# Queries, keys and one mixer's softmax weights: copied bit for bit into float32r row buffers and turned as float32r, with the norm tasks ahead of others

## The chip, the cores and the metric

The kernel runs on one core of one Trainium2 chip. The metric is the device time of one execution in microseconds; the time before is the median of three runs.

## The reference, cut to what matters

One layer of a decoder on a sequence of 512 tokens (S) with a model width of 1024 (D). A combined input projection yields queries, keys and values for two attention mixers of 4 heads with 128 channels each, and gates. Queries and keys pass a per-head RMS norm with a gain and a rotary embedding. The first mixer (DSA) lets each query attend to the 128 keys that a small indexer ranks highest; the second (MoBA) is causal over blocks of 256, which at this size is plain causal attention. Both outputs are projected, gated by sigmoids, added and projected again; a SwiGLU feed-forward layer with 2816 hidden channels follows. Everything is float32.

```python
q_a = apply_rope(rms_norm(q_a.reshape(B, S, DSA_HEADS, HEAD_DIM), g_q_dsa[l]), cos_h, sin_h)
k_a = apply_rope(rms_norm(k_a.reshape(B, S, DSA_HEADS, HEAD_DIM), g_k_dsa[l]), cos_h, sin_h)
o_a = dsa_attention(q_a, k_a, v_a, q_i, k_i, w_i)
q_b = apply_rope(rms_norm(q_b.reshape(B, S, MOBA_HEADS, HEAD_DIM), g_q_moba[l]), cos_h, sin_h)
k_b = apply_rope(rms_norm(k_b.reshape(B, S, MOBA_HEADS, HEAD_DIM), g_k_moba[l]), cos_h, sin_h)
o_b = moba_attention(q_b, k_b, v_b)
# inside both mixers, for every head and block of queries:
#   p = softmax(q @ k.T * scale + mask);  o = p @ v
```

## The kernel before, in words

Large products run on TensorE as float32r in three parts (high times high, high times low, low times high), because every operand is split into a rounded float32r tile and its remainder. The scores (`q @ k.T`) and `p @ v` run as plain float32.

**Queries and keys.** A projection leaves 128 tokens by 512 channels (4 heads) in a PSUM bank. `raw_done` (line 736) has ScalarE copy it into an SBUF tile `raw` of the tag `g` and spawns a task `post` (line 703). There are 16 such tasks: the names `kb`, `qb` (MoBA), `qa`, `ka` (DSA) times 4 blocks of tokens. `post` takes the squares' sums on ScalarE, the rotary embedding on VectorE, the power -1/2 on GpSimd and 4 scalings on ScalarE; then TensorE turns the 4 blocks of 128x128 of `raw` into a PSUM tile `pstr` with float32 transposes (identity `ident` as the moving operand, `raw` as the weights), and ScalarE copies the result into the tile `qk[name]` of the tag `K`.

**Heads.** `head(br, i, h)` (line 881) is one head of mixer `br` (1 is MoBA, 0 is DSA) for the block `i` of 128 queries; its keys reach to the end of that block, so its width is (i+1)*128. There are 16 per mixer. A score product goes to the PSUM tile `pss`; VectorE adds the mask; ScalarE takes the exponential into a tile `p` of the tag `s`; VectorE inverts the sum; ScalarE scales `p`; TensorE turns its i+1 blocks with float32 transposes into `pstr`; ScalarE copies that into `pT`; TensorE multiplies with the values into `pspv`; ScalarE and VectorE store the output in two parts.

**Float32r transposes that are there already.** `flip` (line 777), for the indexer's queries and keys: tiles that ScalarE and VectorE wrote as float32r are turned with `identr`, 4 blocks per call, 8 calls. `ident` is the same tile as `identr`, read as float32.

**The order.** Instructions on TensorE, ScalarE, VectorE and GpSimd run in the order in which the program emits them. A planner writes that order: `Clocks` (line 54) keeps an estimated time for each engine and for each tile. The main stream `drive` (line 586) emits the projections' products; after nearly every triple of products it calls `step` (line 503), which continues every waiting task whose needs are met at the planned time of TensorE. A need is a tile (ready time plus 0.25 us, `when`, line 489), a free buffer of a tag (`room`) or a named event. Tasks are tried in the order of their rank (lower first, 2 by default, in order of spawning within a rank). The main stream goes through MoBA's values, its queries, DSA's queries, keys and values, the gates (16 tiles of the tag `g`), then the two mixers' output projections. These need `attn1` and `attn0`, that is, all heads of a mixer.

**Buffers.** There are 16 tiles of `g`, 4 of `K`, 3 of `s`, 2 of `pT`, 2 banks of `pstr`, 1 each of `pss` and `pspv`.

**DMA.** Weights are loaded on SyncE's queue (`wload`, line 184 issues them), in the order of the tasks. GpSimd's queue issues copies later in the kernel. ScalarE's queue issues none.

Of the kernel before, what the change touches and what calls it, by code (L numbers as in the profile page):

```python
# [23 lines left out]
F32 = mybir.dt.float32  # L24
F32R = mybir.dt.float32r
# [4 lines left out]
P = 128  # L30
S = 512
# [3 lines left out]
HD = 128  # L35
NH = 4
# [81 lines left out]
def layer(ctx, tc, x, vecs, w_mod, w_in, gvecs, w_br_dsa, w_br_moba, w_out, w_gate_up, w_down, cosh, sinh, cosi, sini, out):  # L118
    nc = tc.nc
    ck = Clocks()  # L120
    te, se, ve, ge = (Noted(e, ck) for e in (nc.tensor, nc.scalar, nc.vector, nc.gpsimd))
# [15 lines left out]
    def taken(tag, tile):  # L137

        if free:
            times = free[tag]  # L140
            first = min(times)
            times.remove(first)
            tag_of[tile.tensor.name] = tag
            ck.last[tile.tensor.name] = (first, None)
        return tile

    def done(*tiles):
        for tile in tiles:
            name = tile.tensor.name
            free[tag_of.pop(name)].append(ck.last[name][0])  # L150

    def t(tag, shape, dt=F32):
        uid[0] += 1
        return taken(tag, reg.tile(shape, dt, name=f"{tag}_{uid[0]}", tag=tag, bufs=NB[tag]))

    def small(shape, dt=F32, bufs=4, tag=None):
        uid[0] += 1
        tag = tag or "m" + "_".join(str(v) for v in shape)
        return sm.tile(shape, dt, name=f"{tag}_{uid[0]}", tag=tag, bufs=bufs)
# [3 lines left out]
    def ps(tag, shape=(P, 512), dt=F32):  # L163
        uid[0] += 1
        return taken("ps" + tag, pp.tile(list(shape), dt, name=f"ps{tag}_{uid[0]}", tag="ps" + tag, bufs=NPB[tag]))
# [67 lines left out]
    identr = cp.tile([P, P], F32R, name="identr")  # L233
    ident = identr.bitcast(F32)
# [13 lines left out]
    def rstd_of(ms, width):  # L248

        r = small([P, width])  # L250
        ve.tensor_scalar(r, ms, EPS, None, op0=ALU.add)
        ge.tensor_tensor(out=r, in0=r, in1=mhalf[:, :width], op=ALU.pow)
        return r
# [232 lines left out]
    def room(tag, n=1):  # L486
        return lambda: sorted(free[tag])[n - 1] if len(free[tag]) >= n else None
# [9 lines left out]
    def spawn(gen, slack=2.0, rank=2, on=busy):  # L497
        tasks.append([gen, (), slack, on, rank])
        tasks.sort(key=lambda task: task[4])
# [46 lines left out]
    def need_room(tag):  # L546
        pump(lambda: free[tag])
# [126 lines left out]
    def gain_tables(g):  # L674
        cg = t("cg", [P, NT, HD])
        sg = t("cg", [P, NT, HD])
        hd = HD // 2
        gv = gains[:, g:g + 1, :]
        ve.tensor_tensor(out=cg, in0=cosd, in1=gv.to_broadcast([P, NT, HD]), op=ALU.mult)
        ve.tensor_tensor(out=sg[:, :, 0:hd], in0=sind[:, :, 0:hd],  # L680
                         in1=gv[:, :, hd:].to_broadcast([P, NT, hd]), op=ALU.mult)
        ve.tensor_tensor(out=sg[:, :, hd:], in0=sind[:, :, hd:],
                         in1=gv[:, :, 0:hd].to_broadcast([P, NT, hd]), op=ALU.mult)
        return cg, sg

    def rope(src, cos, sin, heads, d):

        u = t("gu", [P, heads, d])
        hd = d // 2
        ve.tensor_tensor(out=u[:, :, 0:hd], in0=src[:, :, hd:d], in1=sin[:, :, 0:hd], op=ALU.mult)  # L690
        ve.tensor_tensor(out=u[:, :, hd:d], in0=src[:, :, 0:hd], in1=sin[:, :, hd:d], op=ALU.mult)
        yield
        ve.tensor_tensor(out=src, in0=src, in1=cos, op=ALU.mult)
        ve.tensor_tensor(out=src, in0=src, in1=u, op=ALU.add)
        done(u)


    m1 = cp.tile([P, 256], F32, name="m1")
    sqj = m1[:, :HD]
    tabs = {}  # L700
    qk = {}

    def post(name, g, i, raw):
        if not i:
            yield room("cg", 2), room("K")
            tabs[name] = gain_tables(g)
            qk[name] = t("K", [P, NH, S])
            ready.add("tab" + name)
        yield "tab" + name, raw, room("gu")
        if name == "kb" and i >= 2:  # L710
            yield "idx", room("gu")
        cg, sg = tabs[name]
        ss = small([P, NH])
        for h in range(NH):
            se.activation(sqj, raw[:, h, :], AF.Square, scale=HD ** -0.5, accum_out=ss[:, h:h + 1])
        for _ in rope(raw, cg[:, i:i + 1, :].to_broadcast([P, NH, HD]), sg[:, i:i + 1, :].to_broadcast([P, NH, HD]),
                      NH, HD):
            yield ss, cg, sg
        r = rstd_of(ss, NH)
        yield raw, r  # L720
        for h in range(NH):
            se.activation(raw[:, h, :], raw[:, h, :], AF.Copy, scale=r[:, h:h + 1])
        yield raw, room("pstr")
        pt = ps("tr", (P, NH, P))
        for h in range(NH):
            te.transpose(pt[:, h, :], raw[:, h, :], ident)
        se.copy(qk[name][:, :, i * P:(i + 1) * P], pt)
        done(pt, raw)
        ready.add(f"{name}{i}")
        if all(f"{name}{j}" in ready for j in range(NT)):  # L730
            ready.add(name)
            done(*tabs[name])
            if name == "ka":
                done(cosd, sind, gains)

    def raw_done(name, g):
        def fin(i, acc):
            need_room("g")
            raw = t("g", [P, NH, HD])
            se.copy(raw, acc.rearrange("p (h d) -> p h d", h=NH))  # L740
            spawn(post(name, g, i, raw))
        return fin

    vals = {}
# [136 lines left out]
    def head(br, i, h):  # L881
        if br:
            yield "qb", "kb", "vb"
            q, k, v, mask = qk["qb"], qk["kb"], vals["vb"], cmask[:, (NT - 1 - i) * P:]
        else:
            yield ("index", "qa", "ka", "va", "started1") + ((f"bias{i}",) if i else ())
            q, k, v, mask = qk["qa"], qk["ka"], vals["va"], bias[i]
        w = (i + 1) * P
        sl = slice(i * P, (i + 1) * P)
        yield q, k, v, mask, room("pss"), room("s")  # L890
        s_ps = ps("s")
        te.matmul(s_ps[:, :w], q[:, h, sl], k[:, h, :w], start=True, stop=True)
        p = t("s", [P, S])
        st = small([P, 4], tag="att")
        nm, z, rz = (st[:, q:q + 1] for q in range(3))

        ve.tensor_tensor_reduce(out=p[:, :w], in0=s_ps[:, :w], in1=mask, op0=ALU.add, op1=ALU.min, scale=-SCALE,
                                scalar=-LOW, accum_out=nm)
        done(s_ps)
        yield st, p  # L900
        se.activation(p[:, :w], p[:, :w], AF.Exp, bias=nm, scale=-1.0, accum_out=z)
        yield p
        ve.reciprocal(rz, z)
        yield st
        se.activation(p[:, :w], p[:, :w], AF.Copy, scale=rz)
        yield p, room("pstr"), room("pT")
        pt = ps("tr")
        for j in range(i + 1):
            te.transpose(pt[:, j * P:(j + 1) * P], p[:, j * P:(j + 1) * P], ident)
        pT = t("pT", [P, S])  # L910
        se.copy(pT[:, :w], pt[:, :w])
        done(pt, p)
        if br not in outs:
            yield room("O", 2)
            outs[br] = [t("O", [P, NH, S], F32R) for _ in range(2)]
            ready.add(f"started{br}")
        yield pT, room("pspv")
        oh, ol = outs[br][0][:, h, sl], outs[br][1][:, h, sl]
        o_ps = ps("pv", (P, P))
        for j in range(i + 1):  # L920
            te.matmul(o_ps, v[:, j, h * HD:(h + 1) * HD], pT[:, j * P:(j + 1) * P], start=(j == 0), stop=(j == i))
        se.copy(oh, o_ps)
        done(pT)
        yield outs[br][0]
        ve.tensor_tensor(out=ol, in0=o_ps, in1=oh.bitcast(F32), op=ALU.subtract)
        done(o_ps)
        heads.remove((br, i, h))
        if not any(b == br for b, _, _ in heads):
            ready.add(f"attn{br}")
            done(vals["vb" if br else "va"], qk["qb" if br else "qa"], qk["kb" if br else "ka"])  # L930
            if not heads:
                done(cmask, bias[NT - 1])
# [97 lines left out]
    landed = [0.0]  # L1030
# [859 lines left out]
    with tc.manual_schedule(engines=engines):  # L1890
# [20 lines left out]
        for br, i, h in list(heads):  # L1911
            spawn(head(br, i, h), slack=2.5)
# [58 lines left out]
```

## Time and profile before

| what | value |
|---|---|
| time, median of three runs | 767.47 us (767.23 to 768.8) |
| the profiled execution | 767.38 us, of which the span from first to last instruction is 765.6 us |
| TensorE busy | 756.6 us (99%), 3884 products |
| VectorE busy | 603.6 us (79%) |
| ScalarE busy | 413.1 us (54%) |
| GpSimd busy | 62.1 us (8%) |
| granted TensorE clock | 1.000 |
| DMA | 137.10 MB, mean 179 GB/s |

The span is cut by engine: the share of an engine is the time in which at least one of its instructions is running. Products on TensorE overlap, so a group's mean duration is longer than the spacing of its instructions; the spacing of starts is what TensorE's time is made of. Nearly all instructions bear line 111, which is the helper that notes them for the planner, so groups are told apart by the tiles they write and read: `out<-in`, for a product first the moving operand, then the weights. A name without a number stands for all tiles of that tag.

### The profile page before, as it was taken

The page shows a single profiled execution, that of the slowest core. Times are in us where ns is not written, and L with a number is a line of the kernel's source. Part 1 is how long each engine was busy: PE and PEld are TensorE (multiplying, and loading weights), DVE is VectorE, ACT ScalarE, POOL GpSimd, SP SyncE. Part 2 cuts the span into 40 slices and gives each one's busy share as a digit, 9 for nine tenths or more (in the row PEclk, how much of TensorE's full clock was granted, in tenths as well). Part 3 has the DMA queues.
Part 4 walks back from the last instruction along what each step waited for, and adds up shares of the span by engine and source line. Part 5 has one row for each costly group of instructions (what it writes and reads, how often), then busy time and mean ns, then how long its engine had stood idle before and what let it go on. Part 6 is the DMA issues. An engine that isn't in the chain of part 4 may idle for free.

```text
span 765.6 us, 10985 instructions
## 1 busy us (share of the span) xinstructions
PE 756.6 (99%) x3884; PEld 639.2 (83%) x3884; DVE 603.6 (79%) x1183; ACT 413.1 (54%) x887; POOL 62.1 (8%) x91
## 2 busy tenths in 40 slices
PE   7999999999999999999999999999999999999998
PEld 6887888888788887888888988889999998888886
DVE  6974889989799796436967897878788856997896
ACT  6763686869877666643534443444444432554431
POOL 2000012011012000000000000000011020012100
PEclk9999999999999999999999999999999999999999
DMA  9976343542126455534450146744566679579882
GB/s 311 347 215 228 97 167 83 146 133 57 51 65 210 125 153 179 176 92 129 147 157 1 56 148 200 236 164 133 182 204 186 196 250 379 186 264 407 309 310 82
DMA packets 87921, 137.10 MB, mean 179 GB/s; under 512 B 9008, under 2 KB 49272, under 8 KB 87228
## 3 DMA queue, kind: packets, MB, share of 16 engines
q1 hardware_dynamic: 80076, 105.75, 44.0%
q0 software_dynamic: 7792, 30.67, 11.2%
q8 instruction: 30, 0.49, 0.3%
q14 instruction: 23, 0.19, 0.1%
HBM read 117.52 MB, written 18.88 MB: 178 GB/s over the span
## 4 chain that ended last, share of the span: by engine, by line
PE 95%; SPq 2%; DVE 1%; DMA 1%; issue 0%; ACT 0%; ACTq 0%
PE psacc L111 62%; PE pstr L111 11%; PE pspv L111 11%; PE pss L111 11%; SPq L184 1%; DMA K<-in_w_mod_dram 1%; DVE V L111 1%; DVE s L111 1%; SPq L213 0%; SPq L222 0%; ACT gu L111 0%; ACT H L111 0%; SPq L206 0%; ACT acol L111 0%; ACT mcol L111 0%
## 5 line engine op out<-in xcount | busy, mean ns | idle before, releaser
L111 DVE TENSOR_TENSOR wl<-st,wh 128x1024 fp32r<-128x1024 f32 (+1 forms) x98 | 113.6, 1160 | 42.9 <-ACT wh L111 33.6
L111 PE MATMUL psacc<-wh,H 128*128 128x512 f32 x384 | 126.4, 400 | 0.9 <-ACT H L111 0.9
L111 ACT CAST wh<-st 128x1024 fp32r<-128x1024 f32 (+1 forms) x98 | 97.6, 998 | 49.4 <-DMA st<-in_w_gate_up_dram 20.3
L111 PE MATMUL psacc<-H,wh 128*128 128x512 f32 x384 | 124.1, 404 | 0.0
L111 PEld LDWEIGHTS psacc<-wh,H 128*128 128x128 f32 x384 | 72.0, 188 | 16.4 <-ACT H L111 1.4
L111 PEld LDWEIGHTS psacc<-H,wh 128*128 128x128 f32 x384 | 70.0, 188 | 15.3 <-issue 2.7
L111 PE MATMUL psacc<-H,wl 128*128 128x512 f32 x192 | 75.1, 391 | 0.0
L111 PE MATMUL psacc<-H,O 128*128 128x256 f32 (+1 forms) x465 | 72.3, 296 | 0.0
L111 PE MATMUL psacc<-wl,H 128*128 128x512 f32 x192 | 71.0, 390 | 0.0
L111 PEld LDWEIGHTS psacc<-H,O 128*128 128x128 f32 x465 | 64.0, 191 | 2.7
L111 POOL TENSOR_TENSOR m<-m,mhalf 128x4 f32<-128x4 f32 (+1 forms) x24 | 28.6, 1193 | 390.8 <-DVE m L111 356.8
L111 PE MATMUL psacc<-K,O 128*128 128x256 f32 x288 | 43.4, 283 | 0.0
L111 PEld LDWEIGHTS psacc<-H,wl 128*128 128x128 f32 x192 | 36.0, 188 | 7.9
L111 PEld LDWEIGHTS psacc<-wl,H 128*128 128x128 f32 x192 | 36.1, 188 | 6.7
L111 PE MATMUL pss<-H,wh 128*128 128x512 f32 x128 | 39.5, 390 | 0.0
L111 PE MATMUL pspv<-H,wh 128*128 128x512 f32 x128 | 39.5, 390 | 0.0
L111 PE MATMUL psacc<-O,wh 128*128 128x512 f32 x128 | 39.4, 389 | 0.0
L111 PEld LDWEIGHTS psacc<-K,O 128*128 128x128 f32 x288 | 38.4, 191 | 0.0
L111 ACT ACTIVATE s<-s,att 128x256 f32<-128x256 f32 (+3 forms) x64 | 34.2, 562 | 4.6 <-DVE att L111 4.4
L111 ACT CAST H<-st 128x512 fp32r<-128x512 f32 (+1 forms) x21 | 16.1, 766 | 27.5 <-PE psacc L111 26.9
L111 ACT CAST O<-pT 128x512 fp32r<-128x512 f32 x24 | 14.7, 621 | 25.2 <-DVE pT L111 24.7
L111 PEld LDWEIGHTS pspv<-H,wh 128*128 128x128 f32 x128 | 24.0, 188 | 5.1
(338 smaller groups left out, 1628.7 us busy)
## 6 DMA issues: line engine op xcount, KB each, us to landing
st<-in_w_in_dram SPq DMA_DIRECT2D x36, 512.0 KB, 3.5
K<-in_w_mod_dram SPq DMA_DIRECT2D x12, 1024.0 KB, 7.0
st<-in_w_gate_up_dram SPq DMA_DIRECT2D x24, 512.0 KB, 3.9
st<-in_w_down_dram SPq DMA_DIRECT2D x22, 512.0 KB, 4.6
st<-in_w_gate_up_dram SPq DMA_DIRECT2D x40, 256.0 KB, 3.6
K<-in_w_mod_dram SPq DMA_DIRECT2D x16, 512.0 KB, 6.1
O<-second POOLq DMA_DIRECT2D x6, 768.0 KB, 7.0
st<-in_w_in_dram SPq DMA_DIRECT2D x16, 256.0 KB, 4.2
```

What stands on the lines that cost most here:

```text
L111: inst = f(*args, **kw)
L184: last_dma[0] = nc.sync.dma_start(st[:, :, o:o + n], src.rearrange("(k p) n -> p k n", p=P))
```

## The change: what it does

A new function `same_bits` takes a float32 tile, allots a float32r tile of the tag `g`, and issues a DMA on ScalarE's queue that copies the tile's bits into it. For the planner, ScalarE takes 0.1 us for that, and the copy has landed 3.5 us later; until then neither tile is free.

`post` now waits for a free `g` after the scalings, copies `raw`, gives `raw` back, waits for the copy and turns it as float32r (`identr`, a float32r PSUM tile). `head` does the same with `p` for mixer 1 (MoBA) alone; the DSA heads keep the float32 transposes. The `post` tasks get the rank 1.9, ahead of the default 2.

```diff
+    def same_bits(src):
+
+        dst = t("g", [P, 512], F32R)
+        flat = src.rearrange("p h d -> p (h d)") if len(src.shape) == 3 else src
+        nc.scalar.dma_start(dst[:, :flat.shape[1]].bitcast(F32), flat)
+        act = mybir.EngineType.Activation
+        ck.at[act] = max(ck.at[act], ck.ready[src.tensor.name][0]) + 0.1
+        landed = ck.at[act] + 3.5
+        ck.ready[dst.tensor.name] = (landed, None)
+        ck.last[dst.tensor.name] = ck.last[src.tensor.name] = (landed, None)
+        return dst
...
-        yield raw, room("pstr")
-        pt = ps("tr", (P, NH, P))
+        yield raw, room("g")
+        bits = same_bits(raw)
+        done(raw)
+        yield bits, room("pstr")
+        pt = ps("tr", (P, NH, P), F32R)
         for h in range(NH):
-            te.transpose(pt[:, h, :], raw[:, h, :], ident)
-        se.copy(qk[name][:, :, i * P:(i + 1) * P], pt)
-        done(pt, raw)
+            te.transpose(pt[:, h, :], bits[:, h * HD:(h + 1) * HD], identr)
+        se.copy(qk[name][:, :, i * P:(i + 1) * P], pt.bitcast(F32))
+        done(pt, bits)
...
-            spawn(post(name, g, i, raw))
+            spawn(post(name, g, i, raw), rank=1.9)
...
+        if br in (1,):
+            yield p, room("g")
+            bits = same_bits(p[:, :w])
+            done(p)
+            yield bits, room("pstr"), room("pT")
+            pt = ps("tr", dt=F32R)
+            for j in range(i + 1):
+                te.transpose(pt[:, j * P:(j + 1) * P], bits[:, j * P:(j + 1) * P], identr)
+            pT = t("pT", [P, S])
+            se.copy(pT[:, :w], pt[:, :w].bitcast(F32))
+            done(pt, bits)
+        else:
...
```

## Rows read from the trace of the kernel before

**Rows 1.** The page's first part: busy us (share of the span), instructions

```profile
PE 756.6 (99%) x3884; PEld 639.2 (83%) x3884; DVE 603.6 (79%) x1183; ACT 413.1 (54%) x887; POOL 62.1 (8%) x91
```

**Rows 2.** Waits of TensorE, whole span: us in total, times, longest us

```profile
PE pstr L111 <- DMA pT<-in_vecs_dram: 2.7, 1, 2.7
...
PE pstr L111 <- DVE O L111: 0.7, 2, 0.4
```

**Rows 3.** Timeline of TensorE around four float32 transposes: start us, us

```profile
157.80 0.39 PE L111 MATMUL psacc<-wh,H 128*128 128x512 f32 x1
158.03 0.60 PE L111 MATMUL pstr<-identr,g 128*128 128x128 f32 x4
158.38 0.48 PE L111 MATMUL psacc<-wh,H 128*128 128x512 f32 x1
158.70 0.39 PE L111 MATMUL psacc<-wl,H 128*128 128x512 f32 x1
```

**Rows 4.** Timeline of TensorE around four float32r transposes (`flip`)

```profile
84.40 0.46 PE L111 MATMUL pstr<-identr,g 128*128 128x128 f32 x4
84.69 0.46 PE L111 MATMUL psacc<-wh,H 128*128 128x512 f32 x1
85.00 0.40 PE L111 MATMUL psacc<-wl,H 128*128 128x512 f32 x1
```

**Rows 5.** Timeline of TensorE around eight float32r transposes (two calls of `flip`)

```profile
94.68 0.79 PE L111 MATMUL pstr<-identr,g 128*128 128x128 f32 x8
95.31 0.47 PE L111 MATMUL psacc<-wh,H 128*128 128x512 f32 x1
95.62 0.40 PE L111 MATMUL psacc<-wl,H 128*128 128x512 f32 x1
```

**Rows 6.** TensorE's instructions on `pstr`: count, ns min/median/max, first and last start

```profile
L111 PE MATMUL pstr<-identr,s x112: 270/272/273, 167.9 to 423.8; 128*128 128x128 f32 x112
L111 PE MATMUL pstr<-identr,g x96: 221/272/274, 84.4 to 248.4; 128*128 128x128 f32 x96
```

**Rows 7.** Stretches: us, busy of PE, PEld, DVE, ACT, POOL, clock, DMA share, GB/s

```profile
60.00:160.00 100.00, 100.00 (x488) 82.27 (x487) 85.32 (x175) 66.36 (x179) 12.59 (x8) 1.00 0.46 144
160.00:230.00 70.00, 70.00 (x369) 56.91 (x367) 60.18 (x172) 56.67 (x167) 6.97 (x6) 1.00 0.24 65
230.00:308.00 78.00, 78.00 (x407) 63.62 (x406) 64.53 (x165) 53.04 (x141) 3.99 (x3) 1.00 0.53 168
```

**Rows 8.** SyncE's queue, two issues: start us, us on the queue

```profile
113.68 0.25 SPq L1007 DMA_DIRECT2D turned<-K  x1
114.03 0.37 SPq L184 DMA_DIRECT2D st<-in_w_in_dram  x1
```

**Rows 9.** DMA issues by tile: count, KB each, median us from issue to landing

```profile
K<-in_w_mod_dram SPq DMA_DIRECT2D x16, 512.0 KB, 6.1
...
pT<-in_w_down_dram SPq DMA_DIRECT2D x9, 256.0 KB, 2.5
...
out_dram<-V SPq DMA_DIRECT2D x7, 256.0 KB, 2.0
```

**Rows 10.** Timeline of ScalarE: scalings of a head's `p` and of a `raw`

```profile
176.82 0.52 ACT L111 ACTIVATE s<-s,att 128x256 f32<-128x256 f32 x1
...
246.21 1.28 ACT L111 ACTIVATE g<-g,m 128x128 f32<-128x128 f32 x4
```

**Rows 11.** Timeline of TensorE: the transposes that follow these two

```profile
177.74 0.38 PE L111 MATMUL pstr<-identr,s 128*128 128x128 f32 x2
...
248.07 0.60 PE L111 MATMUL pstr<-identr,g 128*128 128x128 f32 x4
```

**Rows 12.** Timeline of ScalarE: the last head's output, and the last gates' first copy

```profile
308.65 0.27 ACT L111 CAST O<-pspv 128x128 fp32r<-128x128 f32 x1 [1.63 <-PE pspv L111]
...
325.52 0.59 ACT L111 COPY g<-psacc 128x512 f32<-128x512 f32 x1 [5.41 <-PE psacc L111]
```

More of the change, by code (lines that the diff above doesn't have):

```diff
@@ L905, in head @@
         se.activation(p[:, :w], p[:, :w], AF.Copy, scale=rz)
[L906 to L912, printed above, removed]
+        if br in (1,):
[10 more added lines that the diff above has]
+        else:
+            yield p, room("pstr"), room("pT")
+            pt = ps("tr")
+            for j in range(i + 1):
+                te.transpose(pt[:, j * P:(j + 1) * P], p[:, j * P:(j + 1) * P], ident)
+            pT = t("pT", [P, S])
+            se.copy(pT[:, :w], pt[:, :w])
+            done(pt, p)
         if br not in outs:
```

## The prediction

> **What bounds the kernel now.** I read the page's first part, then the waits of TensorE alone, then its timeline where the change touches it, then busy times by stretch. The reader should see that TensorE is busy for 756.6 of 765.6 us [rows 1], and that its waits are four rows from 2.7 down to 0.7 us, 5.4 us in all [rows 2], all in the start-up before the projections. In the three stretches where the change lies, 60 to 308 us, TensorE is busy for the whole length of each at clock 1.00 [rows 7]. So nothing waits on the path except for TensorE's own instructions: time is saved only where TensorE has less to do, and any wait that the change brings into TensorE's queue is added in full. ScalarE has room on average (54%), but not everywhere: 66% from 60 to 160 us and 81% from 160 to 230 us [rows 7]. The DMA engines are at 0.46 and 0.24 there.
>
> **Part 1: the transposes.** Starts, not durations, count. Consecutive products of 512 columns start 0.23 us apart (157.80 to 158.03) [rows 3]. Four float32 transposes start at 158.03; the product after them seems to start at 158.38, but the next one is held to 158.70, so the group with one product takes 0.67 us and the four transposes 0.67 - 0.23 = 0.44 us, 0.11 us each. The same sum for float32r: 85.00 - 84.40 - 0.23 = 0.37 us for four, 0.0925 us each [rows 4]; for eight, 95.62 - 94.68 - 0.23 = 0.71 us, 0.089 us each [rows 5]. So float32r is worth only about 0.02 us per transpose. It does not halve it.
>
> How many: 16 `post` tasks with 4 blocks are 64; these are the 96 of `pstr<-identr,g` less 32 of `flip` (8 calls of 4). MoBA's heads have 1+2+3+4 blocks for 4 heads, 40; with as many for DSA and 32 of the later norm they are the 112 of `pstr<-identr,s` [rows 6]. So 104 change. The sum: 16 groups by 0.44 - 0.37 = 0.07 us is 1.1 us; 40 by 0.11 - 0.09 = 0.02 us is 0.8 us; 1.9 to 2.0 us saved on TensorE, nothing beside it. I take 2.0. Bounds: if only the starts inside the group counted, the saving would be 158.38 - 158.03 against 84.69 - 84.40, 0.06 us per four, 104/4 by 0.06 = 1.6 us; if the hold behind float32r vanished where other products follow, 0.11 - 0.29/4 = 0.0375 us each, 3.9 us. A reason excludes a loss here: both forms are measured in this trace, in the same place between the same products.
>
> The Trainium skill has a rule that speaks against this term. "TensorE: Matmul & The Clock Gate", section "LDWEIGHTS (loading the stationary operand)", gives a weight load as the number of columns divided by 1.2, in ns, whatever the format: 107 ns for 128 columns, an estimate from the page. If a short transpose were bound by that in both formats, float32r would save some 0.002 us by 104, 0.2 us. The float32 rows agree with it (110 ns), the float32r rows (89 to 93 ns) do not, and the measurement decides.
>
> **Part 2: the copies on ScalarE's queue.** 32 DMAs: 16 of 256 KB, and four each of 64, 128, 192 and 256 KB, 6.5 MB in all. No row shows an issue on ScalarE. On SyncE an issue takes 0.25 us for a small one and 0.37 us for 512 KB [rows 8]; I take 0.31 us, between the two, and add 0.1 us for the issue's wait until the last scaling has been written, a guess between nothing and the 0.32 us of one whole scaling (1.28/4 [rows 10]). The bounds are 0.25 and 0.5 us; an issue can't take less than nothing. At 0.4 us, 32 make 13 us of ScalarE; the planner counts 0.1 us each, so ScalarE runs up to 0.3 us behind plan after each. Behind each issue on ScalarE's queue stand the weights' high parts, the copies that empty the projections' banks and other heads' exponentials. About 24 of the 32 (MoBA's 16 heads and, if rank 1.9 pulls them forward, the 8 of DSA's queries and keys) fall into 160 to 230 us, where ScalarE idles for 70 - 56.7 = 13.3 us [rows 7]; 24 by 0.4 = 9.6 us fit, but barely.
>
> **Part 3: the wait for the copy.** A transpose now comes at least 0.1 + 3.5 + 0.25 = 3.85 us after the scaling in the planner's time. TensorE fills that with projections and gates, so this delay alone costs nothing, provided that the copy has landed. Landing is not shown for a copy from SBUF to SBUF; the nearest rows are 2.0 us (256 KB out of SBUF) and 2.5 us (256 KB into SBUF); a 512 KB load that comes in twos takes 6.1 us [rows 9]. I take 2.5 us, the row of that size into SBUF, since the DMA engines are half idle; with the issue's own wait some 3.0 us after the scaling. Real time was also ahead of plan before: a head's transposes started 0.40 us after its scaling ended (176.82 + 0.52 against 177.74), those of a key 0.58 us (247.49 against 248.07), where 0.25 was planned [rows 10, 11]. So a typical copy has a microsecond to spare, and one that shares the engines with a pair of large loads (late by up to 6.1 + 0.1 - 3.85 - 0.3 = 2 us) would be rare at a DMA share of 0.24. I put 0.3 us on all such waits together for the likeliest case.
>
> **Part 4: order and buffers.** Rank 1.9 moves norm work ahead of heads; TensorE's own work stays the same, so it costs nothing as long as there is other work. A head holds its `s` tile (3 in all) for 3.6 us longer, so MoBA's heads end later, and the tile `K` for DSA's keys with them. What hides it: the last head ended at 308.65 us, and the last gates are still being emptied at 325.52 us [rows 12], so attention may end up to some 17 us later before TensorE runs dry. The 6.5 MB of copies delay weight loads by less than 1 us each; loads run two chunks ahead. Cost zero.
>
> **Sum.** Against the profiled execution: 767.4 - 2.0 + 0.3 = 765.7 us. That execution (767.38) and the median (767.47) are 0.1 us apart, so this is also the prediction against the median: 0.23% faster. A measurement of this kernel tells a change of 0.2%, 1.5 us, from none, so the forecast lies just across that line.
>
> **Rivals.**
> (a) *ScalarE gives it back.* In 160 to 230 us ScalarE goes from 81% to (56.7 + 9.6)/70 = 95%, and its lag of 0.3 us behind plan exceeds the 0.15 to 0.33 us by which real time was ahead. If half of the 32 copies cost TensorE 0.1 us, 1.6 us are gone: 767.0 us; the span of this case is 766 to 769. For it: that stretch. Against it: 13.3 us idle there, and no wait of TensorE before.
> (b) *Slower: copies land late.* The mechanism is the DMA engines: copies queue among weight loads (6.1 us in [rows 9]) and TensorE stands at a transpose that its fixed order has already reached. It decides from a mean wait of (2.0 + 1.5)/32 = 0.11 us per copy; with 10 copies late by 0.6 us it is 767.4 - 2.0 + 6 = 771.4, with 32 late by 0.15 us 770.2. I take 770.5. Against it: the DMA share of 0.24 in the stretch with most copies.
> (c) *TensorE saves nothing*, both formats being bound alike: 767.2 us. The rows of part 1 speak against it. This is what the page's weight-load rule would make of it.
> (d) *More saved*: the 3.9 us bound, 763.5 us.
>
> **How the numbers follow.** Forecast (765.0 to 765.9) 0.46, (a) 0.33, (b) 0.14, (c) 0.03, (d) 0.04. Faster by over 0.2% (below 765.9): 0.46 + 0.04 = 0.50. Within 0.2%: 0.33 + 0.03 = 0.36. Slower: 0.14. The range for 8 in 10 leaves out most of (b) above and half of (d) below: 764.0 to 769.3. The forecast's own range, 765.0 to 765.9, stands beside it, since cases of both signs take much of the chance.
>
> **What would show it.** Part 1: in the profile after, four `pstr` transposes and the two products after them span 0.60 us instead of 0.67, and `pstr<-identr,s` falls to 72 rows while `pstr<-identr,g` grows to 136. Part 2: issues on ScalarE's queue of about 0.3 us, and ScalarE near 95% where MoBA's heads lie. Part 3: landings of 2 to 3 us and no row of TensorE waiting for a DMA on `g` of over 0.5 us in all. Part 4: the last `O<-pspv` before 325 us. The prediction is wrong if TensorE's waits grow by more than 1.5 us, or if transposes on copied tiles are spaced otherwise than those of `flip`.

## The result and the profile after

| kernel | median (range, runs) | ratio [95% interval] |
|---|---|---|
| before | 768.03 us (767.23 to 768.95, 6) | |
| changed | 772.63 us (771.63 to 775.58, 6) | 1.0069 [1.0051, 1.0087] |

The change makes the kernel 0.7% slower; 0.23% faster was forecast, and 769.3 was the upper end of the range. The profiled execution took 772.36 us, its span 770.2, against 767.38 and 765.6 before.

The page's first part of the changed kernel, to be read against [rows 1]:

```profile
PE 757.5 (98%) x3884; PEld 638.3 (83%) x3884; DVE 604.8 (79%) x1183; ACT 416.3 (54%) x887; POOL 60.6 (8%) x91
```

The work is the same; the span has grown and TensorE's share has fallen. So the loss is time in which TensorE stands. Its waits over the whole span (total us, times, longest us), against [rows 2]:

```profile
...
PE pspv L111 <- DVE O L111: 2.3, 1, 2.3
...
PE pstr L111 <- DMA g<-g: 0.7, 1, 0.7
PE pss L111 <- DVE att L111: 0.7, 1, 0.7
...
```

The four rows left out are the start-up's and were there before. New are 2.3, 0.7 and 0.7 us, 3.7 in all; only one of these, the `g<-g`, is a transpose that waits for its copy. By stretches (us, busy of PE, PEld, DVE, ACT, POOL, clock, DMA share, GB/s), against [rows 7]:

```profile
60.00:160.00 100.00, 99.27 (x483) 81.39 (x482) 79.95 (x163) 66.68 (x177) 10.88 (x8) 1.00 0.45 143
160.00:230.00 70.00, 70.00 (x352) 57.02 (x351) 61.92 (x176) 50.91 (x141) 6.23 (x4) 1.00 0.45 136
230.00:308.00 78.00, 74.90 (x376) 59.85 (x375) 59.51 (x141) 50.36 (x139) 4.78 (x4) 1.00 0.54 176
```

TensorE idles for 0.7 us in the first and 3.1 us in the last. ScalarE, which was to reach 95% from 160 to 230 us, is at 50.91/70 = 73% there, less than before: a busy time leaves DMA issues out, and the work behind the copies has moved to later. With the 17 issues that lie in this stretch, 8.5 us, it is 85%.

One more difference is no part of the change: from 14 to 18 us, in instructions that are the same, this execution had a granted clock of 0.80 and reached the projections 1.4 us later (first `pstr<-H,wh` at 61.5 against 60.1 us). Executions of the kernel before show a lower clock too: of 76 taken here, 40 had a mean clock of 1.000 (median 767.39 us) and 29 one of 0.998 (768.75 us), while of the changed kernel's six none had 1.000 and three, the profiled one among them, had 0.998 (771.87 us), 3.1 us more at the same mean clock. From the first `pstr<-H,wh` to the end, the two profiles read (before, changed; columns as above):

```profile
60.11:765.60 705.49, 701.78 (x3609) 593.31 (x3607) 558.26 (x1089) 372.53 (x812) 57.42 (x79) 1.00 0.52 169
61.55:770.20 708.65, 701.01 (x3609) 591.09 (x3607) 559.34 (x1089) 375.66 (x812) 55.89 (x79) 1.00 0.55 178
```

So of the 5.0 us between the two profiled executions 3.2 are spent here, all at full clock: TensorE is busy for 0.8 us less and idle for 3.9 us more. Another 1.4 us is the start-up's, and 0.4 us lies outside the span.

**The long wait.** TensorE's timeline around it (start us, us):

```profile
300.42 0.93 PE L111 MATMUL psacc<-H,wh 128*128 128x512 f32 x2
301.19 0.40 PE L111 MATMUL psacc<-H,wl 128*128 128x512 f32 x1
303.85 0.71 PE L111 MATMUL pspv<-pT,V 128*128 128x128 f32 x4 [2.27 <-DVE O L111]
```

It waits for VectorE to read the previous `pspv`. VectorE at that time:

```profile
302.06 1.54 DVE L111 SCALAR_TENSOR_TENSOR cg<-K,cs,cg 128x512 f32<-128x512 f32 x2 [2.39 <-DMA K<-in_w_mod_dram]
303.51 0.28 DVE L111 TENSOR_TENSOR O<-pspv,O 128x128 fp32r<-128x128 f32 x1
```

VectorE takes its instructions in the order written: its `O<-pspv` comes at 303.51 us, behind the sums. Ahead of the `O<-pspv` that TensorE needs stands a sum for the modulation row `cg`, which has nothing to do with attention and waits for a load of `w_mod` into a tile `K`. SyncE's queue shows why the load is late:

```profile
292.54 0.37 SPq L184 DMA_DIRECT2D st<-in_w_br_moba_dram  x1
293.15 0.24 SPq L1034 DMA_DIRECT2D turned<-K  x1
296.06 0.37 SPq L1035 DMA_DIRECT2D mcol<-turned  x1
296.48 1.90 SPq L976 DMA_DIRECT2D K<-in_w_mod_dram  x2
```

The reload `mcol<-turned` must wait until the small store `turned<-K` has landed. The store, 2 KB, was issued 0.6 us behind a 512 KB load, and its reload follows 2.91 us after it; in the kernel before, the first such pair stood 1.15 us apart (113.68 to 114.83), and the other three no more than 1.16. The load of `K` stands behind both on SyncE's queue. So: store behind load, reload behind store, load behind reload, VectorE behind load, TensorE behind VectorE.

The `pss` wait of 0.7 us, at 288 us, has the same chain behind it, at the pair before this one. SyncE and then VectorE there:

```profile
276.25 0.24 SPq L1034 DMA_DIRECT2D turned<-K  x1
280.15 0.37 SPq L1035 DMA_DIRECT2D mcol<-turned  x1
280.57 0.50 SPq L976 DMA_DIRECT2D K<-in_w_mod_dram  x1
```

```profile
286.45 0.75 DVE L111 SCALAR_TENSOR_TENSOR K<-K,cs,K 128x512 f32<-128x512 f32 x1 [1.44 <-DMA K<-in_w_mod_dram]
```

The pair stands 3.90 us apart, VectorE waits 1.44 us for the load behind it, and only then, at 287.91 us, reads the tile `pss` that TensorE needs free for its next scores. So 3.0 of the 3.7 us of new waits are the chain's.

**The transposes.** The same kind of place as in [rows 3], now on a copied tile:

```profile
152.70 0.45 PE L111 MATMUL pstr<-identr,g 128*128 128x128 f32 x4
152.99 0.46 PE L111 MATMUL psacc<-wh,H 128*128 128x512 f32 x1
153.29 0.40 PE L111 MATMUL psacc<-wl,H 128*128 128x512 f32 x1
```

The counts that answer to [rows 6], with first and last start:

```profile
L111 PE MATMUL pstr<-identr,g x136: 221/246/412, 85.8 to 280.4; 128*128 128x128 f32 x136
...
L111 PE MATMUL pstr<-identr,s x72: 270/272/273, 286.0 to 428.5; 128*128 128x128 f32 x72
```

Four float32r transposes and the next product take 0.59 us where float32 took 0.67 [rows 3]. That is the saving that was forecast for a group of four.

**The copies.** The issues on ScalarE's queue (ns min/median/max, first and last start) and the time from issue to landing of all:

```profile
L702 ACTq DMA_DIRECT2D g<-g x16: 472/472/572, 102.3 to 275.1; - x16
L702 ACTq DMA_DIRECT2D g<-s x16: 472/472/613, 178.3 to 244.9; - x16
...
DMA to landing us min/median/max: 1.8/2.5/6.0
```

An issue takes 0.47 to 0.61 us; 0.31 was taken and 0.5 was the bound. The median landing is the 2.5 us that was taken; the longest is 6.0 us.

**Attention.** ScalarE's rows that answer to [rows 12]; the first is the last gate copy, the second the last head's output:

```profile
331.06 0.60 ACT L111 COPY g<-psacc 128x512 f32<-128x512 f32 x1
...
337.85 0.27 ACT L111 CAST O<-pspv 128x128 fp32r<-128x128 f32 x1 [1.05 <-PE pspv L111]
```

Attention ends 29.2 us later than before, beyond the cover of 17 us. Yet the view of waits lists none of TensorE's from 305 to 345 us: there was other work for that too.

### The profile page after: what moved, and what is told of

It reads as the page before. It is cut to its first block, busy times and chain, and to the rows that moved or that the text cites. A ratio compares the mean times of both kernels' runs of the same rounds, so it can differ in the third digit from the quotient of the medians.

```text
span 770.2 us, 11089 instructions
## 1 busy us (share of the span) xinstructions
PE 757.5 (98%) x3884; PEld 638.3 (83%) x3884; DVE 604.8 (79%) x1183; ACT 416.3 (54%) x887; POOL 60.6 (8%) x91
## 4 chain that ended last, share of the span: by engine, by line
PE 93%; DMA 3%; DVE 2%; ACT 1%; issue 0%; SPq 0%; DVEq 0%; ACTq 0%
PE psacc L111 61%; PE pstr L111 11%; PE pspv L111 11%; PE pss L111 10%; DMA K<-in_w_mod_dram 2%; DMA g<-g 1%; DVE s L111 1%; DVE V L111 1%; DMA cg<-in_vecs_dram 0%; DMA turned<-K 0%; DVE cg L111 0%; SPq L222 0%; ACT H L111 0%; DVE K L111 0%; ACT s L111 0%
## 5 line engine op out<-in xcount | busy, mean ns | idle before, releaser
L111 PE MATMUL psacc<-H,wh 128*128 128x512 f32 x384 | 126.6, 411 | 0.0
L111 POOL TENSOR_TENSOR m<-m,mhalf 128x4 f32<-128x4 f32 (+1 forms) x24 | 27.0, 1124 | 397.1 <-DVE m L111 391.0
L111 DVE CUSTOM_DVE_ANT_0 s<-pss,sc 128x128 f32<-128x128 f32 (+3 forms) x24 | 11.8, 490 | 22.3 <-PE pss L111 22.2
```

Source lines behind the costliest of these rows:

```text
L111: inst = f(*args, **kw)
```

## The experiments

Each was timed against the kernel before on the same chip (its median there in brackets); all diffs are against the changed kernel unless another is named.

**First group: one part at a time.** The theory of this group and the next was that the moved order costs the time, by way of the late end of attention.

*e1_f32_turn*: the same copies in the same order, float32 transposes.

```diff
-        dst = t("g", [P, 512], F32R)
+        dst = t("g", [P, 512])
...
-            te.transpose(pt[:, h, :], bits[:, h * HD:(h + 1) * HD], identr)
+            te.transpose(pt[:, h, :], bits[:, h * HD:(h + 1) * HD], ident)
```

> The changed kernel with the same copies and the same order of every instruction on every engine, but the copied tiles are declared float32 and turned with float32 transposes. My step (a transpose is worth 0.02 us): 104 transposes cost 2.0 to 2.2 us more, so 774.7 us, and TensorE's waits stay where they are. Rival (float32r saves nothing where the tile came by DMA): the changed kernel's 772.6 us. Rival (float32r halves a transpose): 772.6 + 5.6 = 778.

Measured: 773.67 us (768.7), ratio 1.0073 [1.006, 1.0085]. The place shown above, in this kernel:

```profile
152.93 0.60 PE L111 MATMUL pstr<-identr,g 128*128 128x128 f32 x4
153.28 0.48 PE L111 MATMUL psacc<-wh,H 128*128 128x512 f32 x1
153.60 0.40 PE L111 MATMUL psacc<-wl,H 128*128 128x512 f32 x1
```

0.67 us, against 0.59: at this place float32r does what was forecast for it. The medians differ by 1.0 us and not by the 2.0 to 2.2 expected, and the ratios to the kernel before, 1.0073 and 1.0069, cannot be told apart. The two profiles can: from the first `pstr<-H,wh` on, TensorE is busy for 702.51 us here and 701.01 us in the changed kernel, so all 104 transposes are worth some 1.5 us. A single transpose, as in the heads of the first block of queries, saved nothing: in three of the four it is 0.29 us to the second product behind it in both. The long wait is here too, 2.3 us.

*e2_pool_reload*: the four reloads on GpSimd's queue.

```diff
-        nc.sync.dma_start(mcol[:, j0:j0 + 4], turned.rearrange(...
+        nc.gpsimd.dma_start(mcol[:, j0:j0 + 4], turned.rearrange(...
```

> The changed kernel, the four reloads of the modulation columns (`mcol<-turned`) issued on GpSimd's queue instead of SyncE's; TensorE, VectorE and ScalarE keep their order. Theory (a moved order: attention ends 21 us later and meets the sums over w_mod, whose load stood behind that reload on SyncE's queue): the wait of 2.3 us of TensorE near 301 us goes, 770.3 us. Rival (the copies themselves cost the time, by landing late or by ScalarE's issue time): no change, 772.6 us.

Measured: 771.3 us (768.7), 1.0037 [1.0025, 1.005]. The long wait falls from 2.3 to 1.4 us only: the tile `K` itself is not free until the store has landed (SyncE waits 2.6 us for that before it issues the load), so the load still comes late. A wait of 1.1 us for a copy appears elsewhere. It is a pointer to the chain, not yet a proof.

*e3_rank_only* is the kernel before with rank 1.9 alone; *e4_posts_only* copies queries and keys only (`if br in ():`, rank kept); *e7_heads_only* copies MoBA's heads only (posts and rank as before); *e8_no_rank* is the change without the rank.

```diff
-            spawn(post(name, g, i, raw), rank=1.9)
+            spawn(post(name, g, i, raw))
```

> The kernel before with rank 1.9 for the norm tasks alone, no copies. Theory (moved order; here the last product of attention stands at the 1352nd product, before at the 1399th, changed at the 1507th): no new wait, 768.0 us within 0.5. Rival (the rank is what moves attention into the w_mod sums): 770 us or more.

Measured: 768.73 us (768.7), 1.0011 [0.9999, 1.0024]: the rank alone costs nothing that shows.

> The changed kernel with the copies of queries and keys (16) and the rank, the heads as before. Theory (moved order; attention's last product is the 1374th): no new wait of over 0.5 us but a late copy, 64 transposes save 1.3 us: 766.7 to 767.3 us. Rival (each copy costs TensorE its share of the 5.3 us of waits, 0.17 us): 16 of them cost 2.7 us less 1.3 us, 769.4 us.

Measured: 769.5 us (768.7), 1.0019 [1.0006, 1.0032]: the rival's 769.4, not the theory's 766.7 to 767.3.

> Copies for MoBA's 16 heads alone, norm tasks as before, default rank. Attention ends at product 1370. Theory: 40 transposes save 0.8 us, late copies give back about as much, 768 us within 0.7. Rival (each copy costs its share of the 5.3 us, 0.17 us): 768.5 + 2.7 - 0.8 = 770.4 us.

Measured: 772.42 us (767.72), 1.0065 [1.0045, 1.0086], slower than both expectations. Its profiled execution, the fastest of its six (769.78 us), has one new wait, 1.7 us for a copy, and not the long one. So in another order the copies cost as much as the whole change by way of their own lateness; what the rest is was not settled.

> The changed kernel without rank 1.9. Attention ends at product 1501, as late as in the changed kernel. Theory: 771.5 to 773.5 us. Rival (the rank is what moves it): 768 us.

Measured: 768.17 us (767.72), 1.0005 [0.9992, 1.0018]. This felled the theory's path: here attention ends 24 us later than before (last `O<-pspv` at 332.94 us) and nothing is lost. Late attention is not the cost. At the last pair the store is issued 3.0 us behind the same load of `st` (294.86 against 291.82 us) instead of 0.6 us, and its reload follows 1.15 us after it instead of 2.91. The load of `K` goes out at 296.43 us, no earlier than in the changed kernel, but in this order VectorE does not wait for it.

**Second group: the allowance for landing.** e5_plan_3_0 and e6_plan_2_6 lower the planner's 3.5 us; the edit of e6 is shown, that of e5 has 3.0.

```diff
-        landed = ck.at[act] + 3.5
+        landed = ck.at[act] + 2.6
```

> The changed kernel with all 32 copies; the planner is told that a copy lands after 3.0 us instead of 3.5. Its order comes out otherwise: the turning of DSA's keys ends at product 1216 (changed 1278, before 1140), attention at 1415 (changed 1507, before 1399). Theory (what costs is that attention comes late, because DSA's keys waited for a tile K): TensorE's waits near 280 to 320 us go, some for late copies stay, 767 to 769 us. Rival (the copies themselves cost it): 772.6 us or more, since they are given 0.5 us less.

Measured: 776.0 us (767.72), 1.0109 [1.0085, 1.0134]: attention ends 6 us later than before instead of 29, and the kernel is slower still, against the theory and with the rival. TensorE waits 2.4 us for two copies and 1.6 us for ScalarE.

> The changed kernel, the planner told 2.6 us. Here attention stays late (keys to product 1260, attention to 1492). Theory: as slow as the changed kernel, 771 to 774 us, in spite of the smaller allowance going the same way as in the run with 3.0. Rival (a shorter allowance by itself helps, since tiles are held for less time): faster than the run with 3.0. Rival (late copies): 774 us or more, with waits of TensorE for DMA g of 3 us and more.

Measured: 779.78 us (767.72), 1.0152 [1.0132, 1.0172]. This too is the rival's, late copies. TensorE's waits, two rows:

```profile
PE pstr L111 <- DMA g<-s: 4.9, 2, 4.8
PE pss L111 <- DVE att L111: 2.7, 1, 2.7
```

and where the first of these ends, with the stretches around it (columns as above; the figure before the last two is the clock):

```profile
241.90 0.72 PE L111 MATMUL pstr<-identr,g 128*128 128x128 f32 x4 [4.76 <-DMA g<-s]
```

```profile
236.00:243.00 7.00, 2.24 (x11) 1.63 (x11) 5.20 (x10) 1.09 (x2) 0.00 (x0) 0.76 0.78 261
243.00:250.00 7.00, 7.00 (x36) 6.15 (x35) 2.76 (x7) 1.71 (x4) 0.00 (x0) 0.75 0.10 39
```

TensorE stands for 4.8 us at a copy that landed among loads (DMA share 0.78), and then the granted clock is at half level (1.2 instead of 2.4 GHz) for part of two stretches. A mean of 0.75 over 243 to 250 us is 0.25 * 7 = 1.75 us of full-speed time lost; of the stretch before, TensorE had work only from 241.90 us on, so at half level it lost up to 1.1 / 2 = 0.55 us more there: some 2.3 us beyond the wait. In these orders the transposes meet unlanded copies, so late copies can cost much; whether they are what the change itself lost was the next question.

**Third group: copies that nobody waits for.** In *e9_source_turn* every instruction stands in the changed order, the copies are issued, and the transposes (float32) read the tile that was copied. *e11_source_2_6* is the same in the order of e6.

```diff
-            te.transpose(pt[:, h, :], bits[:, h * HD:(h + 1) * HD], identr)
+            te.transpose(pt[:, h, :], raw[:, h, :], ident)
```

*e10_spare_copies* is the kernel before in its own order, with the 32 copies going to device memory, unread and unknown to the planner:

```diff
+        spare(raw)
         yield raw, room("pstr")
...
+        if br in (1,):
+            spare(p[:, :w])
         yield p, room("pstr"), room("pT")
...
+        dst = dp.tile([P, 512], F32, name=f"spare{uid[0]}")
+        nc.scalar.dma_start(dst[:, :flat.shape[1]], flat)
```

> Every instruction in the changed kernel's order, the 32 copies issued at the same places, but the transposes are float32 and read the tiles that the copies were made from, so that no transpose waits for a copy; nothing else reads the copies. To be held against the float32 twin that does read the copies (773.67 us). Theory 'late copies': TensorE's waits on copies, and the half clock and the late engines that come after them, are what the change costs; without them 769.5 us or less (767.5 of before + 0.5 for the rest, at most +2.0). Rival 'order and SyncE chain': of the changed kernel's 5.3 us of waits only 0.9 us was a transpose at a copy, the long ones (2.4 us behind VectorE and a weight load of the tile K) stay: 772.5 to 773 us. Rival 'issue time on ScalarE': the same 772.5 or more.

Measured: 772.47 us (768.54), 1.0063 [1.0049, 1.0078]: as "order and SyncE chain" expected, not as "late copies" did. Against e1 (773.67), reading the copies costs about 1 us (1.2 by the medians, 0.8 by the ratios). Its longest wait after the start-up is again `pspv`, 2.1 us, at 302 us.

> The kernel before in its own order, with the 32 copies of the same tiles and sizes issued on ScalarE's queue at the same places of the tasks, into tiles in device memory that nothing reads; the planner is not told. Theory 'late copies': issue time (32 by 0.5 us) and the 6.5 MB of traffic alone cost little: 767.5 to 769.0 us, no wait of TensorE over 0.5 us that before does not have. Rival 'issue time on ScalarE': 770 us or more, with waits of TensorE on ACT in the stretch of MoBA's heads. Rival 'traffic': 770 us or more, with waits on VectorE or ScalarE behind weight loads.

Measured: 775.38 us (768.54), 1.0097 [1.0083, 1.0111]. A clear miss for the leading theory: copies that no transpose waits for cost the old order 6.8 us. VectorE's row names what lies behind the largest new wait (total us, times, longest us):

```profile
DVE s L111 <- DMA spare<-s: 7.0, 4, 5.5
```

The mask of a later head must not overwrite a tile `s` before the copy has read it; the planner did not know, VectorE stood 5.5 us once, and TensorE 2.5 us behind it.

> As the first of this group, but in the order that the allowance of 2.6 us makes, whose own time was 779.78 us with float32r transposes that read the copies. Theory 'late copies': 771 us or less, since its two long waits (4.9 and 2.9 us) and the half clock after them hang on copies; float32 transposes cost 2.1 us of this. Rival 'order': the order alone is the bad one, 777 us or more.

Measured: 771.98 us (768.54), 1.0061 [1.0045, 1.0078]. In this order late copies were worth some 9 to 10 us (779.78 - 771.98, and 1.5 to 2.1 for float32), nearly as expected, but the order and the unread copies still cost 3.4 us; the expectation's 771 is missed by 1.

*e12_apart_45_35* drops the rank and allows 4.5 us for queries and keys.

> The changed kernel without rank 1.9, and an allowance of 4.5 us for the copies of queries and keys and 3.5 us for the heads' (both 3.5 us without the rank: 768.17 us). Theory 'late copies': the wait for a key's copy at 130 us (1.0 us) goes, and the float32r transposes' 2.1 us show: 766.0 to 767.3 us, faster than before by 0.1 to 0.2%. Rival 'order': another order, another collision: 768 to 772 us.

Measured: 782.45 us (768.54), 1.0191 [1.0163, 1.0219], the slowest of all and beyond both expectations. Waits for two copies are 4.3 us, and VectorE has this row:

```profile
DVE K L111 <- DMA K<-in_w_mod_dram: 8.4, 1, 8.4
```

A larger allowance is no cure: it makes yet another order. *e16_norank_3_8* (no rank, 3.8 us for all) says the same with less.

> The changed kernel without rank 1.9 and with an allowance of 3.8 us instead of 3.5 (768.17 us with 3.5). Theory 'late copies': its waits at copies (1.0 us at 130 us, 1.5 us at 203 us) shrink by up to 0.3 us each: 767.5 us. Rival 'any other order meets other collisions': 769 us or more.

Measured: 770.26 us (768.01), 1.0031 [1.0018, 1.0044], as the rival had it.

**Fourth group: order, issue and traffic apart.** *e13_order_only* is e9 without any copy (the tiles are allotted and stay unwritten), *e14_tiny_copies* issues them for 4 of 128 partitions, and *e15_spare_tiny* does that to e10; the last edit is shown.

```diff
-        nc.scalar.dma_start(dst[:, :flat.shape[1]], flat)
+        nc.scalar.dma_start(dst[0:4, :flat.shape[1]], flat[0:4, :])
```

> The changed kernel's order and planner, float32 transposes of the original tiles, and no copies at all: the tiles that would take them are allotted and left unwritten. Theory 'traffic and issue': without the copies the order is harmless: 768 to 769 us (e9, with copies nobody reads, was 772.47). Rival 'order': 771.5 to 772.5 us, with the wait of some 2 us of TensorE behind VectorE at about 300 us still there.

Measured: 771.43 us (768.01), 1.0044 [1.0028, 1.006]: by 0.1 us below the range of the rival "order", and with its wait. Three quarters of the change's loss are there without one copy. The wait, and the clock around it:

```profile
PE pspv L111 <- DVE O L111: 2.1, 2, 2.0
```

```profile
299.00:303.00 4.00, 2.47 (x12) 1.60 (x11) 1.90 (x5) 2.53 (x6) 0.00 (x0) 1.00 0.97 339
303.00:306.00 3.00, 2.57 (x9) 1.96 (x10) 1.66 (x7) 1.57 (x5) 0.00 (x0) 0.66 0.33 126
306.00:309.00 3.00, 3.00 (x12) 2.32 (x12) 2.93 (x10) 0.88 (x3) 0.00 (x0) 0.77 0.00 0
```

TensorE stands for 2 us, then runs at half level for (0.34 + 0.23) * 3 / 0.5 = 3.4 us, which costs another 1.7 us. Not each execution shows this: four of eleven kept a mean clock of 1.000, with a median of 769.8 us, 2.4 above the 767.39 of the kernel before at 1.000, and e9's profile has a wait of 2.1 us at the same place with the clock at 1.000. So the wait is worth 2.4 us, and the other 1.0 of the 3.4 us between the medians comes from executions at a lower clock.

> As e13, but with the 32 copies issued, each of 4 of the 128 partitions: the issue time on ScalarE's queue is there, 31 of 32 parts of the bytes are not. Theory 'traffic': 768 to 769 us. Rival 'issue': 771 to 772.5 us while e13 is at 768.5. Rival 'order': 772 as e13.

Measured: 773.07 us (768.01), 1.0055 [1.0034, 1.0076]. Its interval covers e13's ratio: issue time, 0.58 us each here, adds nothing that these runs can tell.

> The kernel before in its own order, with the 32 unread copies into device memory (775.38 us in full size) cut to 4 of 128 partitions. Theory 'traffic': the source tiles come free early and the loads aren't disturbed: 768 to 769.5 us. Rival 'issue': 773 us or more, with the waits on ACT at 171 to 203 us as in full size.

Measured: 772.37 us (768.01), 1.0055 [1.0038, 1.0072]. Nearer to the rival: in the old order, where nobody planned for them, issues and landings of next to no bytes cost over 4 us (TensorE waits of 1.1 us on ScalarE and 0.7 us on VectorE, which stood at a tile `s` again for 3.3 us, until its copy had landed); the full bytes add another 2.5 to 3 us.

*e17_order_nochain* (on e13) and *e18_after_nochain* (on the changed kernel) keep every instruction of TensorE, ScalarE and VectorE in place and cut the chain on SyncE. They leave out the second norm's modulation, whose columns are then other numbers, so they show a cause and are no kernels to use:

```diff
-        nc.sync.dma_start(turned, row)
+        nc.sync.dma_start(turned, w_mod[0:1, 0:512])
-        nc.sync.dma_start(mcol[:, j0:j0 + 4], turned.rearrange(...
+        nc.sync.dma_start(mcol[:, j0:j0 + 4], w_mod[0:1, 0:512].rearrange(...
```

> e13 (the changed order, float32 transposes, no copies; 771.43 us), with every instruction of TensorE, ScalarE and VectorE in the same place, but the small store `turned` and the reload of `mcol` read a row of w_mod in device memory instead of the row in the K tile (so the second norm's modulation columns are other numbers): neither the K tile nor SyncE's queue waits for them. Theory 'K load behind the store': the load of K at 296 us is issued some 3 us earlier, the wait of 2.1 us at 301 us falls below 0.5 us, and the half clock after it goes with it: 768.0 to 769.2 us. Rival 'order elsewhere': 770.5 us or more.

Measured: 767.85 us (767.93), 1.0001 [0.9993, 1.001]. SyncE and VectorE at the place:

```profile
291.28 0.37 SPq L184 DMA_DIRECT2D st<-in_w_br_moba_dram  x1
291.89 5.19 SPq L978 DMA_DIRECT2D K<-in_w_mod_dram  x2
```

```profile
298.29 1.52 DVE L111 SCALAR_TENSOR_TENSOR cg<-K,cs,cg 128x512 f32<-128x512 f32 x2
299.72 0.28 DVE L111 TENSOR_TENSOR O<-pspv,O 128x128 fp32r<-128x128 f32 x1
```

Two loads of `K` are merged in the row; the first goes out 4.3 us earlier than in e13 (291.89 against 296.15), VectorE does not stop, and the whole cost of the order is gone: 3.6 us less than e13.

> The changed kernel itself (772.63 us) with the same edit. Theory 'K load behind the store': the wait of 2.4 us at 301 us goes, those at copies (0.9 us at 132 us) and the rest stay: 769.0 to 770.3 us. Rival 'late copies': the copies' waits are the larger part or take its place: 771.5 us or more.

Measured: 767.62 us (767.93), 1.0 [0.9986, 1.0014]. The same edit takes 5.0 us from the changed kernel, more than the 2.3 to 3.6 expected. Here are TensorE's waits in e18 behind the start-up, and then its time from the first `pstr<-H,wh` on, in e17 and in e18:

```profile
PE pstr L111 <- DMA g<-g: 0.9, 1, 0.9
PE pspv L111 <- DVE O L111: 0.4, 1, 0.4
```

```profile
60.69:766.20 705.51, 701.77 (x3609) 593.31 (x3607) 559.36 (x1089) 375.13 (x812) 55.76 (x79) 1.00 0.51 169
59.87:765.50 705.63, 700.46 (x3609) 591.07 (x3607) 559.06 (x1089) 376.00 (x812) 55.84 (x79) 1.00 0.54 179
```

The waits of 2.3 and 0.7 us are gone, and in the profiles this stretch is 3.0 us shorter than in the changed kernel (705.63 against 708.65): that is what the chain cost. The `pspv` wait of 0.4 us is at another place, 314 us. The rest of the 5.0 us is not the chain's as far as the profiles show: the changed kernel's profile lost 1.4 us at the lower clock of the start-up, which e18's did not have, and behind its long wait the clock stayed at full level. Why none of the changed kernel's six executions had a mean clock of 1.000 stays open; none of e3's twelve had it either, and e3's profile has no long wait. Even so e18 only draws level: against its float32 twin e17, TensorE is busy for 1.3 us less and idle for 1.4 us more, 0.9 us for a key's copy and 0.4 us behind VectorE. No version that ran beats the kernel before beyond the noise. The same edit was not timed on the kernel before; TensorE's waits there are all in the start-up, and all four pairs stand 1.15 us apart.

## Why the prediction was wrong

**What bounds the kernel** held: TensorE is the path, and each new wait was paid in full, in e13 and e6 with interest by the clock.

**Part 1** held in its mechanism: 0.59 us where 0.60 was forecast, and 104 transposes moved from `s` and float32 `g` rows to float32r. Its sum was too large: TensorE's busy time fell by 1.3 us (e18 against e17) to 1.5 us (the changed kernel against e1), not by 2.0, which is under its own lower bound of 1.6; the heads' shortest groups saved little or nothing. Rival (c) is refuted by the 0.67 against 0.59 of e1 and the changed kernel. The rule behind it, in the Trainium skill's "TensorE: Matmul & The Clock Gate", section "LDWEIGHTS (loading the stationary operand)", has columns alone in its formula, an estimate of 107 ns for 128 of them; the spacing of float32r in these rows, (0.59 - 0.23) / 4 = 0.09 us, does not agree with it.

**Part 2** took the issue too short, 0.31 instead of 0.47 us and over, but nothing in the planned order hung on it: e14 cannot be told from e13, and ScalarE came to 85% with the issues counted, not to 95%: 17 of them fell into that stretch and not 24. Rival (a) is not what happened. e15 shows what it costs where the order is not made for it.

**Part 3** was mis-sized. The typical landing was right (2.5 us). "0.3 us on all such waits together" measured 0.7 us in the changed kernel's trace, about 1 us between e9 and e1, and 1.4 us of idle time in e18 against e17, waits behind VectorE included: enough to cancel Part 1. The late ones were not rare: of the 32, seven took 3.2 to 5.7 us from issue to last packet, each with 512 to 2034 KB of loads in flight beside it, also where the mean DMA share is low; the other 25 had at most 418 KB beside them. Lateness goes with what is in flight and not with the mean share. The Trainium skill's "DMA: Bandwidth & Descriptors", section "Anatomy of one DMA — SWDGE (gpsimd) path", fits DMAs issued by GpSimd with 2.0 us plus the bytes over 436 GB/s, an estimate of 2.6 us for 256 KB. The copies here were issued by ScalarE; their median, 2.5 us, is near it, and their longest, 6.0 us, is not.

**Part 4 is the step that failed**: "Cost zero". It asked only whether attention would end before TensorE ran out of other work. Attention ended 29 us later and TensorE did not run out; e8 is 24 us late at no cost. But the new order set a different task beside it: the last `turned`/`mcol` pair now stands, behind a 512 KB load, right ahead of the `K` loads for `cg`, and VectorE reaches `cg` before they land. Cutting the chain takes 3.6 us from e13 and 5.0 us from the changed kernel by the medians (e17, e18); in the changed kernel's profile it is 2.3 and 0.7 us of waits, 3.0 us. No row stood behind "less than 1 us each" for what the copies delay, either: the pair at 276 us stands 3.9 us apart in the changed kernel and 2.0 us in e13, without copies. SyncE's queue and the reuse of the tile `K` were the ones to follow, past the moved tasks; the prediction named "the tile `K` for DSA's keys" as late and did not ask who else uses that tag.

The forecast's rival (b), slower by late copies, had the sign and came nearer (770.5) by luck, with mostly the wrong mechanism: a late transfer at which TensorE's fixed order stands, but in the main a weight load rather than a copy. The account, by the two profiled executions (767.38 and 772.36 us): waits by way of the chain +3.0, the wait for a copy +0.7, idle time that the view of waits does not list +0.2, TensorE's busy time -0.8 (float32r's 1.3 to 1.5, less 0.5 to 0.7 that came back and was not traced), the start-up's clock +1.4, outside the span +0.4. The start-up's 1.4 us and the 0.4 us outside the span are not traced to the change; the other 3.2 us lie where it does.

## What to carry to other kernels

Where the order is written out by hand and TensorE has no idle time, a change's price can lie less in the instructions it adds than in the one load, anywhere, that its new order makes late, as here; list every task that shares a queue, a buffer tag or an in-order engine with what moves, and look at which of its transfers stands behind another. A saving of 2 us in many small pieces needs such a proof first. Test the order by itself (same order, none of the work) before blaming the work: it told more here than eight runs that took parts away.

## What the runs showed of the hardware

- A small transfer landed late when a load was just ahead of it: a 2 KB store stood 1.15 us before its reload in all four places of the kernel before, 2.9 us when issued 0.6 us behind a 512 KB load in the changed kernel, and 1.15 us again when issued 3.0 us behind that load (e8). Copies of 64 to 256 KB took 1.8 to 6.0 us.
- A DMA issue on ScalarE's queue took 0.47 to 0.61 us from one SBUF tile to another, and 0.33 us from SBUF into device memory (e10), against 0.25 and 0.37 us for the two on SyncE's [rows 8].
- A wait of 2.0 us in the middle of TensorE's work was followed in e13's profile by 3.4 us at the clock's lower level, and one of 4.8 us in e6 by some 4.6 us of work at that level (0.25 * 7 / 0.5 and 1.1 us); behind 2.3 us in the changed kernel and 2.1 us in e9 the clock stayed up.
- Between neighbouring projections' products, float32r transposes of 128x128 saved 0.02 us each over float32 in a group of four (0.59 against 0.67 us with the next product); a single one saved nothing that shows (0.29 us in both).
